# A decoder trunk on one core: x is loaded first, the warming products are laid out anew, tile 0's shift is summed on the tensor engine, and small modulation operations move to ACT

## The chip, the core and the metric

The kernel runs on one core of one Trainium2 chip. A core has a tensor engine (PE, with its weight loads shown as PEld), a vector engine (DVE), a scalar engine (ACT), a general engine (POOL) and a queue engine (SP) that here only issues transfers. Each engine runs its own instructions in order and waits on semaphores of the others. Sixteen DMA engines move data between HBM and the on-chip memory (SBUF); products land in eight banks of PSUM, which PE alone fills and DVE and ACT read. The metric is the device time of one execution in microseconds, as the median of several runs.

## The reference, cut to what matters

One layer of a conditioned decoder: 512 positions, width 1024. The first stage, the only one that the change touches, is the first normalisation with its modulation and the first 768 columns of the input projection:

```python
cs = jax.nn.silu(c)                                  # c: (1, 1024)
mod = cs @ w_ada[l] + b_ada[l]                       # w_ada: 1024 x 6144
shift1, scale1, gate1, shift2, scale2, gate2 = [m[:, None, :] for m in jnp.split(mod, 6, axis=-1)]
h = _rmsnorm(x, norm1_g[l]) * (1.0 + scale1) + shift1
proj = h @ w_in[l]                                   # w_in: 1024 x 4352
qa, ka, va, qd, kd, vd, ga, gd = jnp.split(proj, points, axis=-1)
```

After it come a sliding-window attention, a differential attention, a gated merge with an output projection, and a gated MLP with a short convolution. All is float32.

## The kernel before, in words

A float32 product is made of three products in a reduced format: each operand is split into a high part (a cast, on ACT) and a low part (the difference, on DVE), and high x high, low x high and high x low are summed in PSUM. The first stage walks over the 1024 inputs of the projection in eight tiles of 128 (k = 0 to 7). For each tile it needs three things:

- the normalised and modulated x, transposed: `hTh[k]` (high) and `hTl[k]` (low), each 128 x 512. x lies as four row tiles `xn[:, t]` of 128 positions; PE transposes the four 128 x 128 pieces into the bank `xt` (`h_turn`, line 312), and ACT applies scale and shift while it reads that bank (`h_tile`, line 317), once into `hTh` and once into the float32 copy `hf`; DVE subtracts (`h_low`, line 321);
- the modulation of these 128 inputs: scale and shift, which are columns of `cs @ w_ada`. DVE multiplies the eight 128-row blocks of `adaw` (scale and shift side by side, 256 wide) with the eight columns of `cs` and sums them into `ac` (`ac_ops`, lines 253, 255, 257). PE then sums over partitions by a product with ones into `pa` (line 264), and DVE makes two columns `mod` out of it (lines 273 and 276);
- the 768 columns of the weights, `w0`, split by ACT (lines 296, 297) and DVE (lines 303, 305).

Then PE makes 18 products for the tile, in three parts of six (`mm_k`, line 327): part 0 is high weights x high h, part 1 low weights x high h, part 2 high weights x low h. They go to six banks `acc6` that stay open over all eight tiles. Between part 1 and part 2 of tile k stand the product `pa` and the modulation of tile k+1; the transposes of tile k+1 are issued before part 0 of tile k.

Ahead of the loop, ACT squares the four row tiles with a sum over the row (`stat`, line 345), POOL takes the power -1/2 (line 174), DVE polishes it (lines 180, 184) and scales the first 256 columns of the row tile (line 352); PE transposes tile 0's pieces one by one (`turn`, line 357) with three warming products behind each (`keep_warm`, line 335; 14 more stand before them). The remaining 768 columns are scaled by ACT inside the loop's first turn (line 375).

The order of work of DVE, ACT and PE in this stage is written out by hand (a manual schedule); POOL's and SP's follow from a planner. All large loads are issued by SP in the order of the program: c, tile 0's adaw (two loads of 512 KiB), x (four of 512 KiB), then w0 and adaw alternating, where each adaw waits for one of two buffers. A load also waits until the eighth load before it has landed. POOL makes the constants (identity, ones, the attention masks `dsw` and `ddf`, the scales `qsc`) at the beginning and clears `va` by a memset (line 435); masks, scales and `va` are used only in the attention stage.

Of the kernel before, what the change touches and what calls it, by code (L numbers as in the profile page):

```python
# [14 lines left out]
P = 128  # L15
D = 1024
# [21 lines left out]
WARM = 14  # L38
# [14 lines left out]
def kernel(  # L53
# [85 lines left out]
    qsc = cpool.tile([P, 4], F32, name="qsc")  # L139
    for i in range(4):  # L140
        nc.gpsimd.memset(qsc[0:64, i : i + 1], 2.0 ** (i - 2))
        nc.gpsimd.memset(qsc[64:128, i : i + 1], 2.0 ** (i + 2))

    dsw = cpool.tile([P, 256], F32, name="dsw")
    nc.gpsimd.iota(dsw, [[1, 256]], base=-128, channel_multiplier=-1, allow_small_or_imprecise_dtypes=True)
    nc.gpsimd.affine_select(dsw, dsw, [[-1, 256]], ALU.is_ge, NEG, base=128, channel_multiplier=1)
    nc.gpsimd.affine_select(dsw, dsw, [[1, 256]], ALU.is_gt, NEG, base=0, channel_multiplier=-1)
    ddf = cpool.tile([P, 512], F32, name="ddf")
    nc.gpsimd.iota(ddf, [[1, 512]], base=-384, channel_multiplier=-1, allow_small_or_imprecise_dtypes=True)
    nc.gpsimd.affine_select(ddf, ddf, [[-1, 512]], ALU.is_ge, NEG, base=384, channel_multiplier=1)  # L150
# [3 lines left out]
    nc.sync.dma_start(crow8, c.rearrange("o (a p) -> (o a) p", p=P))  # L154
# [9 lines left out]
    pc8 = tbank("pc8", (P, 8))  # L164
    nc.tensor.transpose(pc8, crow8, ident[:8, :8])
# [36 lines left out]
    def load_ada(g):  # L202
        k, m = g[0], len(g)
        aw = pp.tile([P, 2, KT, m * P], F32, tag="adaw", bufs=2, name=f"adaw{k}")
        for j, base in ((0, D), (1, 0)):
            nc.sync.dma_start(
                aw[:, j], wada[:, base + k * P : base + (k + m) * P].rearrange("(a p) n -> p a n", p=P)
            )
        adaw[k] = aw

    load_ada(groups[0])
    for t in range(NT):
        nc.sync.dma_start(xn[:, t], xd[t * P : (t + 1) * P, :])
    for g in groups:
        if g[0]:
            load_ada(g)
        for k in g:
            r = raw_tile([P, 768], f"w0_{k}")
            nc.sync.dma_start(r, win[k * P : (k + 1) * P, 0:768])
            w0[k] = r  # L220
# [24 lines left out]
    def ac_ops(gi, lo, hi):  # L245
# [10 lines left out]
        if hi == KT:  # L256
            nc.vector.tensor_add(ac[gi][0], ac[gi][0], ac[gi][1])
# [101 lines left out]
    for t in range(NT):  # L359
# [5 lines left out]
        if t == 1:  # L365
            finish_mod(0, reduce_mod(0))
# [1359 lines left out]
```

## Time and profile before

| | us |
|---|---|
| median of 3 runs | 719.99 (719.83 to 721.53) |
| the profiled execution | 722.67 |
| its span | 720.9 |
| first product of tile 0 (line 327) | 19.63 |
| first product of tile 1 | 25.25 |
| first product of tile 2 | 30.59 |
| first product of tile 7 | 57.08 |

The times in the lower half are positions in the span, from the timeline. In a timeline row the first number is the start, the second the duration of the group, then the engine, the line, the operation, what it writes and reads, and how many; in brackets stands how long the engine was idle before it, and what ended that wait. In a row of windows the engines' busy times of a stretch are followed by the granted PE clock (1.00 is full), the share of the DMA engines' time, and the GB/s that they moved.

### The profile page before, as it was taken

Reading aid. Unit: us, or ns where it says so; the run is one execution under the profiler, and the core shown is the slowest. Engines: PE = TensorE matmul, PEld = TensorE weight load, DVE = VectorE, ACT = ScalarE, POOL = GpSimd, SP = SyncE. Lnnn points to the kernel's source line nnn. Section 1 sums busy time; section 2 is a strip of 40 time slices with the busy share of each in tenths; the row PEclk is TensorE's granted clock in tenths of the full one; section 3 lists DMA queues with packets and bytes.
Section 4 is the critical chain, followed back from the end, with each engine's and each line's share of the span. In section 5 each row is a group of like instructions: output and inputs, shape, how many; then the busy total and the mean of one; then the engine's idle time right before and its main releaser. Section 6 shows DMA issues by size and latency. Waiting matters only on the chain. (4 is left out here: it accounts for less than half of the span.)

```text
span 720.9 us, 11252 instructions
## 1 busy us (share of the span) xinstructions
PE 693.5 (96%) x4172; PEld 604.8 (84%) x4172; DVE 589.0 (82%) x1121; ACT 381.5 (53%) x673; POOL 84.7 (12%) x101
## 2 busy tenths in 40 slices
PE   5998899999999999999999999999999999999994
PEld 5776788877887888888889999999999999778883
DVE  5998777887986674875379899888888999889996
ACT  3644656454554233432358666555656666555662
POOL 4000000000100110000012021111111212640000
PEclk8999999999999999999999999999999999999998
DMA  9886222534634565726827698877879769998502
GB/s 303 287 265 195 71 59 61 175 101 133 176 109 155 181 196 179 234 88 210 248 68 147 152 198 206 200 175 212 198 202 217 162 174 253 206 206 220 181 0 118
DMA packets 117367, 124.70 MB, mean 173 GB/s; under 512 B 4511, under 2 KB 93376, under 8 KB 117312
## 3 DMA queue, kind: packets, MB, share of 16 engines
q1 hardware_dynamic: 98254, 97.71, 42.8%
q0 software_dynamic: 18720, 25.73, 20.9%
q8 instruction: 33, 0.54, 0.3%
q10 hardware_dynamic: 338, 0.54, 0.2%
q14 instruction: 22, 0.18, 0.1%
HBM read 121.85 MB, written 2.11 MB: 172 GB/s over the span
## 5 line engine op out<-in xcount | busy, mean ns | idle before, releaser
L1112 PE MATMUL up<-t,m_whi 128*128 128x256 f32 x528 | 96.1, 283 | 0.0
L1112 PEld LDWEIGHTS up<-t,m_whi 128*128 128x128 f32 x528 | 82.4, 192 | 0.0
L1112 PE MATMUL up<-t,m_wlo 128*128 128x256 f32 x264 | 74.7, 283 | 0.1
L1112 PE MATMUL up<-bh,p_wlo 128*128 128x256 f32 x232 | 65.7, 284 | 0.6 <-DVE p_wlo L1055 0.6
L1112 PE MATMUL up<-bh,p_whi 128*128 128x256 f32 x232 | 65.6, 283 | 0.0
L1112 PE MATMUL up<-bl,p_whi 128*128 128x256 f32 x232 | 65.6, 283 | 0.0
L1112 PEld LDWEIGHTS up<-t,m_wlo 128*128 128x128 f32 x264 | 50.6, 192 | 0.3 <-DVE m_wlo L1055 0.3
L1112 PEld LDWEIGHTS up<-bh,p_wlo 128*128 128x128 f32 x232 | 44.4, 192 | 1.1 <-DVE p_wlo L1055 1.1
L748 DVE SCALAR_TENSOR_TENSOR arow<-ra,cs,arow 128x512 f32<-128x512 f32 x56 | 41.9, 748 | 3.9 <-DMA ra<-in_w_ada_dram 3.3
L1112 PEld LDWEIGHTS up<-bh,p_whi 128*128 128x128 f32 x232 | 44.5, 192 | 0.0
L1112 PEld LDWEIGHTS up<-bl,p_whi 128*128 128x128 f32 x232 | 44.5, 192 | 0.0
L1023 POOL DMA_DIRECT2D s<-in_w_up_dram x21 | 27.2, 1385 | 143.2 <-DMA s<-in_w_up_dram 60.1
L1055 DVE TENSOR_TENSOR m_wlo<-s,m_whi 128x1024 fp32r<-128x1024 f32 x31 | 37.8, 1219 | 2.0 <-ACT m_whi L1051 2.0
L1051 ACT CAST m_whi<-s 128x1024 fp32r<-128x1024 f32 x31 | 32.4, 1047 | 9.4 <-DVE s L1045 6.0
L174 POOL TENSOR_TENSOR r<-ms,mhalf 128x1 f32<-128x1 f32 (+1 forms) x16 | 13.5, 844 | 172.9 <-DVE ms L172 106.0
L1112 PE MATMUL up<-t,p_whi 128*128 128x256 f32 x176 | 32.2, 283 | 0.0
L678 ACT ACTIVATE sd<-sd,dmx 128x128 f32<-128x128 f32 (+3 forms) x32 | 17.8, 556 | 22.1 <-DVE dmx L676 15.6
L761 POOL DMA_DIRECT2D mod_rows<-arow x8 | 4.3, 540 | 205.4 <-ACT arow L760 205.2
L1112 PEld LDWEIGHTS up<-t,p_whi 128*128 128x128 f32 x176 | 27.4, 192 | 0.2 <-issue 0.2
L1119 ACT ACTIVATE gT<-a,cv 128x512 f32<-128x512 f32 x22 | 17.7, 814 | 17.7 <-DVE a L1154 17.3
L1051 ACT CAST p_whi<-wa 128x1024 fp32r<-128x1024 f32 x18 | 18.7, 1041 | 12.1 <-PE up L1112 9.0
L1112 PE MATMUL up<-t,p_wlo 128*128 128x256 f32 x88 | 24.9, 283 | 0.0
(476 smaller groups left out, 2125.3 us busy)
## 6 DMA issues: line engine op xcount, KB each, us to landing
ra<-in_w_ada_dram SPq DMA_DIRECT2D x32, 512.0 KB, 4.2
wa<-in_w_up_dram SPq DMA_DIRECT2D x22, 512.0 KB, 4.3
s<-in_w_up_dram SPq DMA_DIRECT2D x21, 512.0 KB, 4.8
s<-in_w_up_dram POOLq DMA_DIRECT2D x21, 512.0 KB, 6.5
adaw<-in_w_ada_dram SPq DMA_DIRECT2D x16, 512.0 KB, 5.1
w<-in_w_in_dram SPq DMA_DIRECT2D x12, 512.0 KB, 4.6
a<-in_w_up_dram SPq DMA_DIRECT2D x11, 512.0 KB, 4.7
b<-in_w_down_dram SPq DMA_DIRECT2D x10, 512.0 KB, 4.3
```

The costliest lines, as they stand in the source:

```text
L174: nc.gpsimd.tensor_tensor(r0, ms, mhalf[:, :n], ALU.pow)
L678: nc.scalar.activation(pm[m], pm[m], AF.Exp, bias=mx[:, m : m + 1], scale=slope, accum_out=lsum[:, m : m + 1])
L748: nc.vector.scalar_tensor_tensor(ac, r[:, a], cc, ac, ALU.mult, ALU.add)
L761: nc.gpsimd.dma_start(mod_rows[idx : idx + 1, hf * S : (hf + 1) * S], row)
L1023: nc.gpsimd.dma_start(dst, upblock(*blk), accum_op=ALU.add)
L1051: nc.scalar.copy(W[J, name][0], R[J, SRC[name]])
L1055: nc.vector.tensor_sub(lo, R[J, SRC[name]], hi.bitcast(F32))
L1112: nc.tensor.matmul(o[u], w[:, k, cu], b[:, k], start=name in ("p1", "m5", "p2") and k == 0 and x == 0, stop=k == 3 and x == 2, skip_group_ ...
L1119: nc.scalar.activation(grow(j), av[J][:, u], AF.Identity, bias=cv[:, 66 + j : 67 + j], scale=cv[:, 44 + j : 45 + j])
```

## The change

Nothing of the result is computed differently in sense. What moves:

1. SP's order of loads: three row tiles of x, tile 0's scale columns in two halves, the last row tile of x in two halves, tile 0's shift columns in three pieces, w0 of tile 0 in two pieces, tile 1's adaw in four pieces, then as before, but with w0 of tile 2 now standing ahead of tile 2's adaw in the queue. c is loaded over ACT's queue, ahead of the bias rows.
2. The constants for the attention (`qsc`, `dsw`, `ddf`) and the memset of `va` are made after the stage's statistics, as POOL's order is now also written by hand.
3. The warming products use ones for both operands and no longer wait for the identity: 4 before c's transpose, 8 behind it, 4 behind each of the first two x tiles, 2 before the first product, in place of 14 and three times 3.
4. For tile 0, DVE sums only the scale half (128 wide); the shift half is eight products on PE straight from `adaw` with a column of `cs`. For tile 1, the last two of eight blocks of both halves go the same way. `pa` is 48 columns wide instead of 1.
5. The two columns of `mod` are made by ACT, with a new column `cb` = (1 + bias) x gain made once on DVE; the bias and gain columns are prepared later, after the second row tile.
6. The statistics of the last row tile come in two halves; the scaling of the other 768 columns (`scale_x`) is spread over ACT's time ahead of the loop.
7. Tile 0's weights: the high part of the 512 query columns is made by DVE, that of the other 256 by ACT; the products of tile 0 begin with the latter (banks 4 and 5).

```diff
-WARM = 14
...
-    nc.sync.dma_start(crow8, c.rearrange("o (a p) -> (o a) p", p=P))
+    nc.scalar.dma_start(crow8, c.rearrange("o (a p) -> (o a) p", p=P))
...
-    load_ada(groups[0])
-    for t in range(NT):
-        nc.sync.dma_start(xn[:, t], xd[t * P : (t + 1) * P, :])
...
+    adaw[0] = pp.tile([P, 2, KT, P], F32, tag="adaw", bufs=2, name="adaw0")
+    for t in range(NT - 1):
+        load_x(t)
+    for lo in (0, 4):
+        load_ada_part(adaw[0], 0, 0, 1, lo, lo + 4)
+    load_x(NT - 1, (0, S, D))
+    for lo, hi in ((0, 4), (4, 6), (6, 8)):
+        load_ada_part(adaw[0], 1, 0, 1, lo, hi)
+    load_w0(0, (512, 768))
+    load_w0(0, (0, 512))
+    for g in groups[1:]:
+        load_ada(g, (0, 4, 8) if g[0] == 1 else (0, 8))
+        load_w0(g[0])
...
+    def keep_warm(n):
+        for i in range(n):
+            nc.tensor.matmul(acc6[5][:, :P], ones, ones, start=True, stop=True)
+
+    keep_warm(4)
+    pc8 = tbank("pc8", (P, 8))
+    nc.tensor.transpose(pc8, crow8, ident[:8, :8])
...
+        js = slice(0, 1 if gi == 0 else 2)
+        for kk in range(lo, min(hi, KT - direct(gi))):
+            a = ac[gi][kk % 2][:, js]
...
+    def direct(gi):
+        return 2 if gi == 1 else 0
+
+    NB = 48
...
+    def mod_mm(pa, aw, j, lo, hi, start):
         for kk in range(lo, hi):
...
+            nc.tensor.matmul(
+                pa[:, j], aw[:, j, kk], cs[:, kk : kk + 1].to_broadcast([P, NB]),
+                start=start and kk == lo, stop=kk == KT - 1,
             )
...
+    def reduce_one(pa, gi, j):
+        more = direct(gi)
+        nc.tensor.matmul(pa[:, j], ac[gi][0][:, j], ones[:, 0:NB], start=True, stop=not more)
+        mod_mm(pa, adaw[gi], j, KT - more, KT, False)
+
+    def finish_one(k, pa, j):
...
+        if j == 0:
+            nc.scalar.activation(m[:, 0:1], pa[:, 0, 0:1], AF.Identity, bias=cb[:, k : k + 1], scale=n1g[:, k : k + 1])
+        else:
+            nc.scalar.activation(m[:, 1:2], pa[:, 1, 0:1], AF.Identity, bias=bsh[:, k : k + 1])
...
-        for i in range(6):
+        for i in (4, 5, 0, 1, 2, 3) if k == 0 else range(6):
...
+    keep_warm(4)
+    stat(2)
+    scale_x(0)
+    ac_ops(0, 0, 4)
+    normalise(2)
+    turn(2)
+    pa0 = pa_bank(0)
+    ac_ops(0, 4, 6)
+    stat(3)
+    ac_ops(0, 6, KT)
+    scale_x(1)
+    mod_mm(pa0, adaw[0], 1, 0, 4, True)
+    mod_mm(pa0, adaw[0], 1, 4, 6, False)
+    ps0 = acc6[3].rearrange("p (j n) -> p j n", j=2)[:, :, 0:NB]
+    reduce_one(ps0, 0, 0)
+    normalise(3)
+    mod_mm(pa0, adaw[0], 1, 6, 8, False)
+    turn(3)
+    wts[0] = tuple(wp.tile([P, 768], F32R, tag=f"w{b}", bufs=WB, name=f"w0{b}0") for b in ("hi", "lo"))
+    nc.scalar.copy(wts[0][0][:, 512:768], w0[0][:, 512:768])
+    finish_one(0, ps0, 0)
+    finish_one(0, pa0, 1)
+    rq, wq, lq = w0_views(0)
+    nc.vector.tensor_copy(wq, rq)
+    split_lo(0, 1)
     h_tile(0)
+    scale_x(2)
+    scale_x(3)
     split_lo(0, 0)
...
                 h_turn(nxt[0])
+                if gi == 0:
+                    keep_warm(2)
             for part in range(3):
                 if part == MOD_AT and k == g[-1] and nxt:
-                    pas = reduce_mod(gi + 1)
+                    pa = pa_bank(nxt[0])
+                    for j in range(2):
+                        reduce_one(pa, gi + 1, j)
+                    for j in range(2):
+                        finish_one(nxt[0], pa, j)
                     split_lo(nxt[0], 0)
-                    finish_mod(gi + 1, pas)
                     split_lo(nxt[0], 1)
...
+    va = big.tile([P, 2, 4, 2 * P], F32R, tag="kvB", name="va")
+    nc.gpsimd.memset(va.bitcast(F32), 0.0)
     man.close()
```

165 lines of the change are left out of this document (70 added, 95 removed).

## The prediction

> **What bounds the kernel now.** The page comes first. TensorE (PE) is busy nearly all the time, and less so in the first fortieth, 18 us.
>
> ```profile
> span 720.9 us, 11252 instructions
> PE 693.5 (96%) x4172; PEld 604.8 (84%) x4172; DVE 589.0 (82%) x1121; ACT 381.5 (53%) x673; POOL 84.7 (12%) x101
> PE   5998899999999999999999999999999999999994
> ```
>
> The change lies wholly in the first 62 us, so I read that stretch by windows, then by the timeline. In the windows' rows the columns are PE, PEld, DVE, ACT, POOL, then granted clock, DMA share, GB/s.
>
> ```profile
> 0.00:5.00 5.00, 0.42 (x2) 0.35 (x2) 0.83 (x5) 1.60 (x3) 4.02 (x22) 1.00 0.55 158
> 5.00:10.00 5.00, 5.00 (x24) 4.98 (x24) 4.43 (x13) 0.58 (x1) 1.50 (x1) 1.00 1.04 347
> 10.00:15.00 5.00, 2.44 (x18) 2.16 (x17) 2.04 (x12) 4.65 (x10) 1.61 (x3) 0.91 1.08 378
> 15.00:19.60 4.60, 4.30 (x19) 3.92 (x19) 4.38 (x16) 0.99 (x3) 0.98 (x2) 0.50 1.10 339
> 30.20:35.60 5.40, 5.35 (x28) 4.17 (x27) 5.21 (x15) 2.32 (x5) 0.00 (x0) 1.00 0.88 278
> ```
>
> Until 19.6 us the DMA engines are full (share 1.04 to 1.10): loads set the pace. In the loop (last row) DVE works 5.21 of 5.40 us and DMA has room again. The timeline of the start:
>
> ```profile
> 1.18 1.03 SPq L206 DMA_DIRECT2D adaw<-in_w_ada_dram  x2
> ...
> 1.48 0.09 POOL L141 MEMSET qsc<- 64x1 f32 x1
> ...
> 4.70 1.80 POOL L435 MEMSET va<- 128x2048 f32 x1
> ...
> 5.35 1.18 DVE L240 TENSOR_SCALAR cols<-cols 128x8 f32<-128x8 f32 x1
> ...
> 6.91 0.62 DVE L253 TENSOR_SCALAR ac<-adaw,cs 128x256 f32<-128x256 f32 x2 [0.36 <-DMA adaw<-in_w_ada_dram]
> ...
> 9.42 1.06 ACT L345 ACTIVATE sq<-xn 128x1024 f32<-128x1024 f32 x1 [6.65 <-DMA xn<-in_x_dram]
> ...
> 12.81 0.33 PE L357 MATMUL xt<-ident,xn 128*128 128x128 f32 x1 [1.71 <-DVE xn L352]
> ...
> 14.19 0.19 ACT L345 ACTIVATION_READ_ACCUMULATOR sq<-xn 128x1 f32 x1
> ...
> 14.29 0.60 ACT L296 CAST w0h<-w 128x512 fp32r<-128x512 f32 x1
> ...
> 15.16 0.15 DVE L170 TENSOR_SCALAR ms<-ss 128x1 f32<-128x1 f32 x1
> ...
> 16.63 0.35 DVE L352 TENSOR_SCALAR xn<-xn,rst 128x256 f32<-128x256 f32 x1
> ...
> 17.06 1.49 PE L335 MATMUL a<-ones,ident 128*128 128x128 f32 x6
> ...
> 18.55 1.06 PE L312 MATMUL xt<-ident,xn 128*128 128x128 f32 x4
> 18.80 0.78 ACT L317 ACTIVATE hThA<-xt,mod 128x512 fp32r<-128x512 f32 x1 [3.61 <-PE xt L357]
> ...
> 19.63 2.23 PE L327 MATMUL a<-hThA,w0h 128*128 128x512 f32 x6
> ```
>
> ACT sits idle 6.65 us until the first x tile lands, because 1 MiB of adaw stands ahead of it. Then come four squares, the statistics, transposes, hThA, and only at 19.63 the first product. Next, one turn of the loop, and its last two starts:
>
> ```profile
> 24.12 0.61 DVE L253 TENSOR_SCALAR ac<-adaw,cs 128x256 f32<-128x256 f32 x2
> ...
> 28.32 0.58 PE L264 MATMUL pa<-ones,ac 128*128 128x1 f32 x4
> ...
> 30.59 1.64 PE L327 MATMUL a<-hThA,w0h 128*128 128x512 f32 x6
> ...
> 32.06 1.54 PE L327 MATMUL a<-hThA,w0l 128*128 128x512 f32 x6
> ...
> 33.43 0.68 DVE L303 TENSOR_TENSOR w0l<-w,w0h 128x512 fp32r<-128x512 f32 x1
> ...
> 33.66 0.58 PE L264 MATMUL pa<-ones,ac 128*128 128x1 f32 x4
> 34.10 1.63 PE L327 MATMUL a<-hTlA,w0h 128*128 128x512 f32 x6
> 34.27 0.22 DVE L273 SCALAR_TENSOR_TENSOR mod<-pa,cols 128x1 f32<-128x1 f32 x1 [0.16 <-PE pa L264]
> 34.41 0.15 DVE L276 TENSOR_TENSOR mod<-pa,cols 128x1 f32<-128x1 f32 x1
> 34.47 0.42 DVE L305 TENSOR_TENSOR w0l<-w,w0h 128x256 fp32r<-128x256 f32 x1
> 34.65 0.78 ACT L317 ACTIVATE hThA<-xt,mod 128x512 fp32r<-128x512 f32 x1 [3.08 <-DVE mod L276]
> 34.81 0.61 DVE L253 TENSOR_SCALAR ac<-adaw,cs 128x256 f32<-128x256 f32 x2
> ...
> 35.56 0.60 PE L312 MATMUL xt<-ident,xn 128*128 128x128 f32 x4
> 35.92 1.64 PE L327 MATMUL a<-hThA,w0h 128*128 128x512 f32 x6
> ...
> 52.02 1.64 PE L327 MATMUL a<-hThB,w0h 128*128 128x512 f32 x6
> ...
> 57.08 1.56 PE L327 MATMUL a<-hThB,w0h 128*128 128x512 f32 x6
> 58.48 1.56 PE L327 MATMUL a<-hThB,w0l 128*128 128x512 f32 x6
> ```
>
> A turn lasts 5.33 us (30.59 to 35.92). DVE waits only 0.16 us in it (for pa) and is the bound; PE is close behind.
>
> **The change, part by part: loads.** I turn the GB/s rows into bytes moved: 0.79 MB at 5.0, 2.53 at 10, 4.42 at 15, 5.98 at 19.6. One MiB is 1.05 MB. Adaw's first MiB was moved at 5.75 and landed at 6.9, 1.2 us later; the cast of w0 (3.54 MB, moved at 12.7) started at 14.29 without a wait, so its lag was at most 1.6. The changed order starts its large loads at the head of SP's queue, where c stood (c goes to ACT's queue), some 0.4 us earlier. With a lag of 1.2 to 1.6: the last half of x (2.62 MB, moved at 10.2) lands at 11.0 to 11.4; tile 0's shift weights (3.15 MB) at 12.4 to 12.8; w0 (3.54) at 13.5 to 13.9; tile 1's adaw (4.59) at 16.2 to 16.6. Tile 2's adaw comes at 6.42 MB, since w0 of tiles 1 and 2 now go ahead of it: at the 339 GB/s of the row before, moved at 20.9, landed at 21.7 to 22.1; I take 21.9. The pieces are smaller (15 issues in place of 10), but about 1.4 MB is always queued, so I cost the extra issues at nothing.
>
> **Statistics and first product.** x3's two half squares are an estimate of 0.55 us each (half of 1.06). From the last half: square and accumulator read 0.75, to 11.95; ms to the end of the scaled head took 15.16 to 16.98, 1.82, giving 13.8; transposes about 0.6; hThA 0.8 and a handover: 15.2. PE's queue has tile 1's four transposes (1.06) and two warming products ahead of the first product. Three of these took 1.49 at half clock, so two take 0.5 to 1.0, and the first product starts at about 16.1, against 19.63. The squares of x0 to x2 and scale_x(0) and (1) fill ACT's waits for later x tiles. The mod columns are needed on ACT by 14.4; the shift's eight products follow their weights (12.8) by two or three of pa's 0.44 us, so they fit. Making w0's high part on DVE (a 512-wide copy, 0.4 to 0.7 by the 512-wide CAST and TENSOR_TENSOR rows) takes 1.0 us of casts off ACT, less the 256-wide one that stays.
>
> **Tile 1.** DVE after 13.8: copy 0.6, two low parts 1.0, six ac operations 2.2, the low part of h and the sum 1.1: 18.7. PE: 16.1 plus two parts (30.59 to the earliest end of the second, 1.47 + 1.40 = 2.87) is 19.0. pa has six products in place of two, three times 0.44 = 1.3; then 1.46 and 0.36. Tile 1's first product: 22.1, against 25.25.
>
> **Tile 2, where gain is given back.** DVE would be free for ac(2) at 19.7, but adaw lands at 21.9: that is the new wait, behind which h_low and the low parts of w0 queue. From ac(2) to pa took 24.12 to 28.32, 4.2, and from pa to the next tile's start 28.32 to 30.59, 2.27. So tile 2 starts at 28.4, against 30.59: 2.2 us earlier.
>
> **The loop.** Two DVE operations per tile go to ACT. From L303 to L305 it was 1.04 us; without them about the 0.6 that L303's issue needs: DVE's turn falls to 4.9. PE's turn is then the bound: 1.47 + 1.40 (57.08 to 58.48, undisturbed) + 0.44 + 1.46 + 0.36 = 5.13 to 5.15. ACT's two small operations are not in the trace in this form. Nearest below is DVE's 0.15 to 0.22, nearest above the 1.18 that L240 shows; I take 0.2, as both normal neighbours are there. hThA then starts where it did, about 1.0 after pa, and ends 0.4 before PE needs it, so they cost nothing; at over 0.4 each they would show. Each of the four turns from tile 2 to tile 6 gains about 0.2, and the last (52.02 to 57.08 before, 5.06; no transposes in it, 5.15 - 0.36 = 4.79 after) 0.27: 1.0 in all. Wider pa (48 columns) hides in its weight loads.
>
> **Constants.** qsc, dsw, ddf and va's memset, 5.0 us of POOL (1.48 to 6.50 before), now run after x3's power, from about 13.1 to 18.1; nobody needs them before 60 us. The row at 5.35 shows the danger: DVE's 128x8 operation took 1.18 beside va's memset, ending at 6.53, just behind it. At 13.8 to 18.1 DVE's only plain copy falls beside the short qsc memsets, so zero by the near rows, up to 4.3 if everything waits for POOL.
> By the Trainium skill ("SBUF — State Buffer", section "Who interferes with whom"), an operation of DVE that uses both port pairs waits out a GpSimd operation completely, and one with two SBUF inputs waits only for one that reads SBUF. The trace agrees (1.18 beside va). This speaks against moving the constants here, and is a rival below.
>
> **Sum.** 2.2 at tile 2 plus 1.0 in the loop = 3.2 us. What follows (evacuation at 60 us, products that PE bounds) has the same instruction order and moves as a block. The profiled execution took 722.67 us (span 720.9 plus 1.8 around it), 2.7 above the median of 719.99; I carry the difference alone: 719.99 - 3.2 = 716.8.
>
> **Rivals.**
> *The clock stays at half.* The row from 15 to 19.6 shows 0.50, after no wait of PE longer than 1.71 us. The changed PE has waits of that size between transposes. If it is at half clock from 16.1 to 20.6, tile 0's first two parts take 5.1 in place of 2.87: pa(1) at 21.2, tile 1 at 24.4, tile 2 at 29.5 (24.4 + 2.87 + 2.27), and with the loop's 1.0 the gain is 2.1: 717.9. For: the same pattern before. Against: warming products now stand between all transposes.
> By the Trainium skill ("TensorE: Matmul & The Clock Gate", section "Part 1: The HAM clock gate (the "warmup" mystery)") the clock falls only after an idle window of about 3.4 us. By that no gap here would lower it, and the sum stays 716.8. The trace differs: it fell behind gaps of 1.7 us.
>
> *No wait for tile 2's adaw.* If it lands by 19.7, PE bounds tile 1 too (22.1 + 2.87 + 2.27 = 27.2): 1.2 more, 715.6. For: rates of 378 at 10 to 15 us. Against: 339 as soon as adaw is in the stream.
>
> *The constants block DVE.* All of DVE's work after 13.8 waits for 18.1: the sum of tile 1 at 23.0, ac(2) at 23.9, tile 2 at 30.4; gain 0.2 + 1.0: 718.8.
>
> *Slower: the stream of small pieces runs slower.* Place: SP's first 17 loads, each waiting for the eighth before it. The forecast turns into a loss over 0.3% when ac(2) starts after 27.3 (21.9 + 3.2 + 2.2), that is 6.42 MB at under about 270 GB/s from 2.5 us on. At 250 it starts at 29.4 and the time is 724.3. For: 158 in the first five us, and 278 in the loop. Against: in the loop DVE paces the loads; wherever loads were queued, the rows show 339 to 378.
>
> **How the numbers follow.** A measurement of this kernel tells about 0.3%, 2.2 us, from no change. The forecast (716.8, own range 715.9 to 717.8) 0.53; no wait 0.15; half clock 0.15; constants 0.08; slower stream 0.09. Faster: 0.53 + 0.15 = 0.68. Same: 0.23. Slower: 0.09. The range takes in no wait below with 0.4 for the loads' lag, and half clock and constants above: 715.2 to 718.9; left out are the slower stream and some edges.
>
> **What would show it.** x0's square starts at about 5 us, not 9.4; first product at 16, tile 1 at 22, tile 2 at 28.4, tile 7 at 53.8; a DVE wait for adaw of some 2 us before ac(2); turns of 5.15 with PE free of waits; ACT's mod operations 0.2 each. The forecast is wrong if the clock row at 16 to 21 us stays at 0.5, if pieces land at under 300 GB/s, or if the stages after 62 us do not move with the first one.

## The result: slower by 0.44%, and the profile after

The changed kernel takes 724.11 us (721.97 to 726.09) where the kernel before, measured beside it, takes 720.39 (718.76 to 722.46): a ratio of 1.0044 with an interval of 1.0029 to 1.0059. The forecast was 716.8, with a range up to 718.9: the sign is wrong.

The page of the changed kernel (span, engines, and PE's busy tenths in 40 slices):

```profile
span 719.9 us, 11298 instructions
...
PE 694.2 (96%) x4192; PEld 605.4 (84%) x4192; DVE 585.7 (81%) x1106; ACT 386.0 (54%) x690; POOL 84.6 (12%) x101
...
PE   8899899999998999999999999999999999999994
```

The first slice of PE went from 5 to 8 tenths, and the span from 720.9 to 719.9. By these lines the change looks like a small gain. It is not, since the profile of before that I had read was a long execution of that kernel: 722.67 us, where its median is about 720.4. A second profile of it (720.08 us, span 718.3, called "before, again" below) is the fairer partner, with one reserve: at 370 us PE waits 1.68 us for DVE in it, where no other profile loses more than 0.4. Distances to it that are given below for places before 370 us therefore don't add up to the difference of the spans. The start in rows of the timeline, first of the changed kernel:

```profile
4.31 1.06 ACT L354 ACTIVATE sq<-xn 128x1024 f32<-128x1024 f32 x1 [0.69 <-DMA xn<-in_x_dram]
...
13.89 0.35 ACT L289 ACTIVATE mod<-a,cb,cols 128x1 f32<-128x1 f32 x1 [0.91 <-PE a L281]
...
16.28 2.47 PE L341 MATMUL a<-hThA,w0hi 128*128 128x512 f32 x6
...
17.45 1.81 POOL L466 MEMSET va<- 128x2048 f32 x1
...
22.58 0.62 DVE L257 TENSOR_SCALAR ac<-adaw,cs 128x256 f32<-128x256 f32 x2 [2.53 <-DMA adaw<-in_w_ada_dram]
...
23.04 1.66 PE L341 MATMUL a<-hThA,w0h 128*128 128x512 f32 x6
...
27.43 0.35 ACT L289 ACTIVATE mod<-pa,cb,cols 128x1 f32<-128x1 f32 x1 [3.21 <-PE pa L281]
27.68 0.25 ACT L291 ACTIVATE mod<-pa,cols 128x1 f32<-128x1 f32 x1
...
29.03 0.62 DVE L257 TENSOR_SCALAR ac<-adaw,cs 128x256 f32<-128x256 f32 x2 [1.46 <-DMA adaw<-in_w_ada_dram]
...
29.06 1.64 PE L341 MATMUL a<-hThA,w0h 128*128 128x512 f32 x6
...
35.49 1.64 PE L341 MATMUL a<-hThA,w0h 128*128 128x512 f32 x6
...
55.72 1.67 PE L341 MATMUL a<-hThB,w0h 128*128 128x512 f32 x6 [0.21 <-ACT hThB L331]
...
60.65 0.50 PE L117 MATMUL pq<-hThA,w_h 128*128 128x512 f32 x1 [0.46 <-DVE qa L483]
```

and of before, again:

```profile
18.57 1.66 PE L327 MATMUL a<-hThA,w0h 128*128 128x512 f32 x6 [0.43 <-ACT hThA L317]
...
24.04 1.66 PE L327 MATMUL a<-hThA,w0h 128*128 128x512 f32 x6 [0.16 <-ACT hThA L317]
...
29.12 1.64 PE L327 MATMUL a<-hThA,w0h 128*128 128x512 f32 x6
...
34.47 1.64 PE L327 MATMUL a<-hThA,w0h 128*128 128x512 f32 x6
...
55.61 1.58 PE L327 MATMUL a<-hThB,w0h 128*128 128x512 f32 x6
...
60.44 0.50 PE L118 MATMUL pq<-hThA,w_h 128*128 128x512 f32 x1 [0.47 <-DVE qa L428]
```

Tile 0 starts 2.3 us earlier (16.28 against 18.57) and tile 1 1.0; tile 2 starts level (29.06, 29.12) and tile 3 1.0 later. The loop wins most of that back; the first product after the stage stands 0.2 later. The brackets of two rows show why: DVE waits twice for tile weights of the modulation, 2.53 us ahead of tile 2's sums and 1.46 ahead of tile 3's. The windows of the changed kernel (columns as in the prediction):

```profile
10.00:15.00 5.00, 3.36 (x26) 2.85 (x25) 4.71 (x21) 3.44 (x9) 2.47 (x11) 0.97 1.15 308
15.00:20.00 5.00, 5.00 (x22) 4.29 (x20) 5.00 (x11) 3.66 (x6) 4.04 (x6) 0.69 1.11 334
```

and of before, again:

```profile
10.00:15.00 5.00, 2.88 (x21) 2.61 (x20) 2.50 (x16) 4.12 (x8) 2.28 (x4) 0.89 1.09 371
15.00:20.00 5.00, 4.57 (x24) 4.11 (x24) 4.86 (x14) 2.26 (x5) 0.30 (x1) 0.76 1.10 368
```

The DMA engines are as busy as before (1.15 and 1.11 of their time) but move 308 and 334 GB/s instead of 371 and 368. So the stage brings nothing. That explains a missing gain, not a loss of 2 to 3.7 us; the rest had to be found later in the program, where the change edits nothing.

### The profile page after: what moved, and what is told of

The parts are those of the page before. It is cut to its first block, busy times and chain, and to the rows that moved or that the text cites. A ratio compares the mean times of both kernels' runs of the same rounds, so it can differ in the third digit from the quotient of the medians.

```text
span 719.9 us, 11298 instructions
## 1 busy us (share of the span) xinstructions
PE 694.2 (96%) x4192; PEld 605.4 (84%) x4192; DVE 585.7 (81%) x1106; ACT 386.0 (54%) x690; POOL 84.6 (12%) x101
## 5 line engine op out<-in xcount | busy, mean ns | idle before, releaser
L159 POOL TENSOR_TENSOR r<-ms,mhalf 128x1 f32<-128x1 f32 (+1 forms) x16 | 12.7, 795 | 177.3 <-DVE ms L157 107.1
```

Source lines behind the costliest of these rows:

```text
L159: nc.gpsimd.tensor_tensor(r0, ms, mhalf[:, :n], ALU.pow)
```

## The experiments

Two theories stood at first. By the one, the loss arises in the first stage (the order or the pieces of the loads, the constants on POOL, the granted clock). By the other, it arises later, from something that the first stage shifts. The second took shape when I set the same PE instructions of two traces beside each other: in the changed kernel's first profile their distance to before, again hardly moves from 62 to 170 us (0.2 at both ends) and then grows in steps, most of it between 185 and 232 us.

### The same kernels again

before_same is the kernel before, after_same and after_same2 are the changed one, all with no edit.

> The kernel before, unchanged, once more, for the spans and clocks of its executions. Its earlier profile had a span of 720.9 us, 2.3 above what its usual time leaves (720.4 less 1.8). Theory A (what is lost lies behind the first stage, in stretches at half clock): most executions here show a span near 718.6 and a mean clock above the 0.988 of the earlier profile, about 0.992. Theory B (what is lost lies in stages whose pace the loads set): spans near 718.6 with the same clock as the changed kernel's executions, about 0.989.

> The changed kernel, unchanged, once more. 0.3 to 0.6% above the kernel before. Theory A: a second stretch at half clock stands in the clock row of this profile whenever its mean clock is below 0.992, and the instructions behind it come 1.7 to 2.6 us later than in the earlier profile of this kernel. Theory B: the clock row is as in the earlier profile, and the loss lies at 180 to 270 us, in a wait for a load.

> The changed kernel once more, beside the three that differ from it in one part. 722.8 to 724.1 us, mean clock about 0.990; if its profile shows a mean clock of 0.990 or less, then by theory A two or three stretches at half clock stand at 12 to 22 us, and tile 1 starts at 24 to 26 us in place of 23.

Measured: 720.44 us (ratio to the runs beside it 0.9995, 0.9978 to 1.0012); 722.82 (1.0040, 1.0022 to 1.0058); 722.24 (1.0031, 1.0015 to 1.0046). The loss is real and lies between 2.0 and 3.7 us. after_same starts its tiles 0, 1 and 2 at 16.30, 23.06 and 29.67. after_same2 shows, for tile 1, the rival of the half clock as it was drawn up:

```profile
16.99 2.91 PE L341 MATMUL a<-hThA,w0hi 128*128 128x512 f32 x6
...
24.38 1.65 PE L341 MATMUL a<-hThA,w0h 128*128 128x512 f32 x6
...
29.65 1.64 PE L341 MATMUL a<-hThA,w0h 128*128 128x512 f32 x6
```

```profile
13.40:20.00 6.60, 6.49 (x24) 5.62 (x24) 6.12 (x16) 4.86 (x9) 5.23 (x13) 0.50 1.12 324
68.00:71.30 3.30, 3.30 (x17) 2.25 (x16) 2.15 (x13) 0.00 (x0) 0.00 (x0) 0.50 0.54 161
```

The rival had tile 1 at 24.4 and tile 2 at 29.5. That tile 2 agrees too is luck: after_same has a single half-clock window and starts it at 29.67. In both, DVE gets tile 2's adaw only at 23.2 us, and tile 2 starts 6.5 us later. So theory A's marks are there in after_same2 (two windows at 13 to 20 us, tile 1 above 24), and a loss at the place that theory B names is there in after_same (0.9 us between 185 and 232). The half clock itself occurs in some executions and not in others: the mean granted clock is 0.990 and 0.991 over the runs of after_same and after_same2, and 0.993 over those of before_same. A half-clock window of 3.4 us takes 0.0024 off a run's mean, so the changed kernel has on average about one more of them. What that costs stands in the sum at the end of the section on why the prediction was wrong.

### Parts of the change undone or exaggerated

const_early makes POOL's constants and the memset at the beginning, as before:

```diff
+    qsc = cpool.tile([P, 4], F32, name="qsc")
...
+    va = big.tile([P, 2, 4, 2 * P], F32R, tag="kvB", name="va")
...
-    man.enter_context(tc.manual_schedule(engines={nc.vector.engine, nc.scalar.engine, nc.tensor.engine, nc.gpsimd.engine}))
+    man.enter_context(tc.manual_schedule(engines={nc.vector.engine, nc.scalar.engine, nc.tensor.engine}))
...
+    nc.gpsimd.memset(va.bitcast(F32), 0.0)
```

> The changed kernel with the attention's constants and the clearing of va made by POOL where the kernel before made them. By my prediction's step (constants behind the statistics cost nothing) the same as the changed kernel within 0.1%, the ten products before 20 us unmoved. Rival (POOL beside DVE slows the operations of DVE there): ac(1) takes 0.61 per pair in place of 0.96, tile 1 starts 0.5 to 1.0 us earlier, tile 2 not at all, since it waits for its load.

Measured: 722.85 us, 1.0038 (1.0023 to 1.0054), as after_same in the same comparison (722.82). Where the constants stand is worth nothing that can be told from these runs, though the slowdown that the rival fears is there. The first two operations of tile 1's sums on DVE, in the changed kernel beside POOL's work on the constants, and in const_early without it:

```profile
15.28 0.96 DVE L257 TENSOR_SCALAR ac<-adaw,cs 128x256 f32<-128x256 f32 x2
```

```profile
15.95 0.61 DVE L269 TENSOR_SCALAR ac<-adaw,cs 128x256 f32<-128x256 f32 x2
```

From tile 0's start to tile 1's it is 6.76 us in the one and 6.75 in the other.

big_pieces keeps the new order of loads and loads each in one piece:

```diff
-    for lo in (0, 4):
-        load_ada_part(adaw[0], 0, 0, 1, lo, lo + 4)
-    load_x(NT - 1, (0, S, D))
...
+    load_ada_part(adaw[0], 0, 0, 1, 0, 8)
+    load_x(NT - 1)
...
-        load_ada(g, (0, 4, 8) if g[0] == 1 else (0, 8))
+        load_ada(g)
```

> The changed kernel's order of loads, but each in one piece as before (the scale and the shift columns of tile 0, the last row tile, w0 of tile 0, and tile 1's adaw): six loads fewer. My rival of the prediction (small pieces run slower): ac(2) starts before 21.5 us in place of 22.6, and the time falls by 1 us or more. If only the bytes ahead of tile 2's adaw count: ac(2) starts at 22.2 to 22.9 again; tile 0 starts some 0.5 to 1 us later, as its last pieces land later; the time stays within 0.15%.

Measured: 725.74 us, 1.0070 (1.0044 to 1.0096), 2.9 above after_same, though the two intervals just overlap. Tile 2's sums start at 24.08 us, not before 21.5. The small pieces help rather than harm; the rival that the prediction set on the slower side has its sign reversed.

w_behind makes SP issue the loads from tile 1 on in the program's order, so that tile 2's weights no longer stand ahead of its adaw:

```diff
+    inorder = ExitStack()
+    inorder.enter_context(tc.manual_schedule(engines={nc.sync.engine}))
     for g in groups[1:]:
         load_ada(g, (0, 4, 8) if g[0] == 1 else (0, 8))
         load_w0(g[0])
...
+    inorder.close()
```

> The changed kernel with SP's loads from tile 1 on in the order of the program: tile 2's adaw ahead of tile 2's w0, tile 3's ahead of tile 3's and 4's. If the bytes ahead of adaw set the pace of the first tiles: tile 2's adaw lands some 1 us earlier (0.39 MB at 330 GB/s is 1.2), ac(2) starts at 21.4 to 22.2 in place of 22.6 to 23.2, tile 3 at about 34.4 in place of 35.4, and the time falls by 0.5 to 1 us. If not (the loads are slow for another reason, or w0 becomes the late one): tile 3 at 35.4 again and the time within 0.1%.

Measured: 723.36 us, 1.0048 (1.0034 to 1.0062). Tile 2's sums start at 21.81, as the first branch has it, but PE had two half-clock windows (13.5 to 20.3 us) and tile 2 starts at 29.64 all the same. Tile 3 starts at 35.34, as in the changed kernel, and no gain shows. In this profile the clock stands in the way, so the order of these two loads is not tested by itself.

after_warm adds four warming products at three places (behind the third tile's transposes, ahead of the scale sum, behind the last transposes):

```diff
     turn(2)
+    keep_warm(4)
...
     turn(3)
+    keep_warm(4)
```

> The changed kernel with 12 warming products more, four each in TensorE's waits at 11.5 to 14.5 us. Theory A (stretches at half clock cost the changed kernel more than the kernel before; its mean clock was 0.990 against 0.993): no half clock at 14 to 18 us, mean clock up to 0.993 to 0.997, the time 1 us lower. If the clock at the start doesn't matter, since loads set the pace there: the same time within 0.1%, whatever the clock.

Measured: 724.93 us, 1.0065 (1.0042 to 1.0088). The profile shows half clock from 12.2 to 22.5 us. More warming at these places does not hold the clock: the mean over the runs is 0.990, as in after_same.

x_second loads tile 0's adaw ahead of x, with all the rest of the change in place:

```diff
+    for lo in (0, 4):
+        load_ada_part(adaw[0], 0, 0, 1, lo, lo + 4)
+    for lo, hi in ((0, 4), (4, 6), (6, 8)):
+        load_ada_part(adaw[0], 1, 0, 1, lo, hi)
     for t in range(NT - 1):
         load_x(t)
-    for lo in (0, 4):
-        load_ada_part(adaw[0], 0, 0, 1, lo, lo + 4)
     load_x(NT - 1, (0, S, D))
-    for lo, hi in ((0, 4), (4, 6), (6, 8)):
-        load_ada_part(adaw[0], 1, 0, 1, lo, hi)
```

> The changed kernel with tile 0's adaw loaded ahead of x again; all else as changed. By my prediction's step (x first brings the first product 3.5 us forward, and tile 2 2.2 us): tile 0 at 18.5 to 20 us, tile 2 at 30 to 31, time 1.5 to 2.2 us above the changed kernel. By theory E (tile 2's and later starts are set by the bytes ahead of their adaw, which are the same): tile 0 later by 2 to 3 us, tile 1 by 1 to 2, but tiles 3 to 7 within 0.5 us of the changed kernel, time within 0.15% of it.

Measured: 727.29 us, 1.0093 (1.0073 to 1.0113), 5.0 above after_same2 beside it. Its tiles 0 and 1:

```profile
22.81 2.46 PE L341 MATMUL a<-hThA,w0hi 128*128 128x512 f32 x6
...
29.58 1.65 PE L341 MATMUL a<-hThA,w0h 128*128 128x512 f32 x6
```

The start does reach the end: a stage that begins 6 us later costs 5 us. Part of that is clock, since PE does nothing from 7.5 to 10.9 us in this profile, has half clock from 10.9 to 24.6, and the runs' mean clock is 0.987 against 0.991. Both expectations missed, the one of 1.5 to 2.2 us by its size, and the one that nothing would change altogether; with it fell the theory that the first stage is hidden. "x first" is worth having within this change.

### The length of TensorE's program

The change also makes PE's program longer: 45 instructions more in the first stage, 24 of them ahead of the loop. The trace of before shows 33 packets of 16 KB on the queue named q8 instruction, over the whole span. I take them for PE's program, fetched piece by piece: the page counts 8344 products and weight loads on PE, and 33 packets of 256 instructions are 8448. Three kernels test whether the place of these fetches matters. They put products of 8 x 8 numbers, which nobody reads, in front of the warming; as compiled, each is four instructions.

before_pad adds 11 of them to the kernel before (44 instructions, about what the change adds), before_pad32 adds 32 and before_pad64 adds 64 in the same place:

```diff
+    for i in range(11):
+        nc.tensor.matmul(acc6[5][:8, :8], ones[:, :8], ones[:, :8], start=True, stop=True)
```

> The kernel before with 11 tiny products more (8 x 8) ahead of the first warming products, where TensorE waits for the identity: 44 TensorE instructions more, so that the fetches of its program, one of 16 KB for every 256 instructions, fall where they fall in the changed kernel (which has 45 more). Theory C (the stages behind the first lose 2 us because each fetch occupies one DMA engine for about 1 us, and now hits loads on which the end waits): the first stage as before, then TensorE falls behind by 0.4 to 0.6 us at 173, 0.5 at 198, 0.5 to 1.0 at 221 us, and the time rises by 1 to 2 us, to about 721.5 to 722.5. Theory D (those steps come from something else in the changed start): no steps, 720.4 within 0.15%.

> The kernel before with 64 tiny products more at its start, where there were 11: 256 TensorE instructions, one whole block, so that the fetches behind the first stage fall where they fall in the kernel before. Theory C (the place of the fetches costs the time): DVE's waits for the row write of the modulation are three of together 4.4 to 4.6 us again, not four of 6.9 as with 11 products; no steps at 189, 198 and 221 us; 720.4 us, or up to 0.7 less if the clock stays full at the start. Theory D (the added products themselves bring the loss, through the clock or the start): about 722.0 as with 11 of them.

> The kernel before with 32 tiny products at its start: 128 TensorE instructions, half a block. Fetches then fall some 11 us earlier in the work than in the kernel before, about 173 and 195 us in place of 184 and 206, and none stands beside the row write at 180 us. Theory C: DVE's wait behind that row write is 0.3 us as in the kernel before, not 1.9 as with 11 products, no step at 189 us, and the time is 719.5 to 721, unless the fetch hits another transfer that the end waits for. Theory D (any added products that leave the old place cost): 721.5 to 722.5, as with 11.

Measured: before_pad 722.02 us, 1.0019 (1.0009 to 1.0029); before_pad64 720.55, 1.0006 (0.9992 to 1.0020); before_pad32 721.83, 1.0010 (0.9993 to 1.0028). Eleven products of next to no work make the kernel before slower by 1.6 us, and 64 of them by less than can be told; 32 lie between and can't be told from either. With 64 the program is one packet longer, and every later fetch is back in its old place; before_pad, then before_pad64:

```profile
q8 instruction: 33, 0.54, 0.3%
```

```profile
q8 instruction: 34, 0.56, 0.3%
```

What a fetch meets in its new place is a write of 2 KB to HBM (`mod_rows`, a row of the later modulation), for which DVE waits before it overwrites `arow`. The write's issue and DVE's next operation in before_pad:

```profile
180.83 0.55 POOL L763 DMA_DIRECT2D mod_rows<-arow  x1 [11.79 <-ACT arow L762]
...
184.18 0.49 DVE L748 TENSOR_SCALAR arow<-ra,cs 128x512 f32<-128x512 f32 x1 [1.95 <-DMA mod_rows<-arow]
```

in before_pad64:

```profile
181.52 0.55 POOL L763 DMA_DIRECT2D mod_rows<-arow  x1 [11.79 <-ACT arow L762]
...
183.16 0.48 DVE L748 TENSOR_SCALAR arow<-ra,cs 128x512 f32<-128x512 f32 x1 [0.28 <-DMA mod_rows<-arow]
```

and in after_same2:

```profile
180.57 0.55 POOL L815 DMA_DIRECT2D mod_rows<-arow  x1 [11.79 <-ACT arow L814]
...
183.69 0.49 DVE L800 TENSOR_SCALAR arow<-ra,cs 128x512 f32<-128x512 f32 x1 [1.74 <-DMA mod_rows<-arow]
```

That the fetch is what delays the write shows in its parts: in before_pad a fetch starts 1.31 us after the write's issue, 15 of the write's 16 parts land 1.45 to 1.61 us after that issue, and the last at 3.33; in before_pad64 all 16 land by 1.62. DVE waits 1.95 and 1.74 us in place of 0.28, and everything behind that on its queue comes later, up to the operands of four transposes on PE at 222 us. Two groups of products, ahead of the place and behind it, measure what this costs PE; in before, again (170.73 to 222.54, 51.81 us):

```profile
170.73 0.95 PE L125 MATMUL sd<-qkv 64*128 64x128 f32 x12
...
222.54 0.63 PE L693 MATMUL td<-ident,sd 128*128 128x128 f32 x4 [0.33 <-DVE sd L684]
```

in before_pad (53.49 us):

```profile
172.91 0.95 PE L125 MATMUL sd<-qkv 64*128 64x128 f32 x12
...
226.40 0.63 PE L695 MATMUL td<-ident,sd 128*128 128x128 f32 x4 [1.03 <-DVE sd L686]
```

in after_same2 (53.78 us):

```profile
172.62 0.96 PE L124 MATMUL sd<-qkv 64*128 64x128 f32 x12
...
226.40 0.63 PE L747 MATMUL td<-ident,sd 128*128 128x128 f32 x4 [1.52 <-DVE sd L738]
```

The kernel whose only edit is 44 idle instructions loses 1.7 us in this stretch, the changed one 2.0, and both end it on a wait for DVE. before_pad64 loses nothing here (the table below). Its time is a weaker witness than its trace: its runs had a mean clock of 0.9957, against 0.9929 for those beside it, and its profile lies 2.8 us behind before, again already at 100 us. The 64 products may thus cost something at the start and gain something by the clock; no run here tells the two apart. Now the changed kernel with its fetches moved back. after_pad adds 23 and 30 tiny products at two places (212 instructions, 257 with the change's 45; `pad(n)` is n of the products above); tiny, the second diff, puts 65 of them in place of 12 warming products (257 again):

```diff
+    pad(23)
     keep_warm(4)
...
+    pad(30)
     keep_warm(8)
```

```diff
-    keep_warm(4)
     nc.tensor.transpose(pc8, crow8, ident[:8, :8])
+    for i in range(65):
+        nc.tensor.matmul(acc6[5][:8, :8], ones[:, :8], ones[:, :8], start=True, stop=True)
...
-    keep_warm(8)
```

> The changed kernel with 53 tiny products more (8 x 8) among the first warming products: 212 TensorE instructions, which with the 45 of the change make one whole block of 256, so that all later fetches fall where they fall in the kernel before. Theory C: the steps at 173, 198, 221 and 252 us are gone, and the time falls by 1 to 2 us, less what the products cost at the start (0 to 1 us). Theory D: the steps stay; the time stays or rises by up to 1 us.

> The changed kernel with 65 tiny products behind c's transpose in place of the first twelve warming products: the TensorE program is then longer than that of the kernel before by a whole block (257 instructions against 256), and c's columns are not delayed. Theory C: waits for the row write 4.4 to 4.7 us in three, time 1.3 to 1.7 us below the changed kernel of this call, about 721.5. Theory A on top (tiny products at the start went with a clock of 0.993 and more): another 0.5 to 1 us. Neither: as the changed kernel.

Measured: after_pad 722.78 us, 1.0043 (1.0027 to 1.0058): no gain, a miss for the theory. tiny 721.49, 1.0011 (0.9997 to 1.0024), 0.75 below after_same2 beside it, with intervals that overlap, and at a higher mean clock (0.9945 against 0.9907), so that its time alone does not speak for the theory. DVE's wait is back at 0.25 and 0.26, and in tiny the stretch takes 51.85 us again:

```profile
172.45 0.96 PE L124 MATMUL sd<-qkv 64*128 64x128 f32 x12
...
224.30 0.63 PE L747 MATMUL td<-ident,sd 128*128 128x128 f32 x4 [0.32 <-DVE sd L738]
```

In after_pad PE still loses 1.2 us between 185 and 232, at another point (195 to 202); its cause I did not find.

### A third buffer for adaw

Do the two waits for adaw in the first stage come with its two buffers? adaw3 gives the changed kernel three, before_adaw3 the kernel before; adaw3_pad and adaw3_tiny are after_pad and tiny with three, and adaw3_tiny33 has 33 tiny products in place of 65:

```diff
-        aw = adaw[k] = pp.tile([P, 2, KT, m * P], F32, tag="adaw", bufs=2, name=f"adaw{k}")
+        aw = adaw[k] = pp.tile([P, 2, KT, m * P], F32, tag="adaw", bufs=3, name=f"adaw{k}")
```

> The changed kernel with three buffers for adaw in place of two, so that no load of adaw waits for DVE to have read the one before the last, and tile 2's adaw stands ahead of tile 2's w0 in the queue. Theory E (the first stage is bound by the loads of adaw, and that is where the 3.2 us of my sum went): no DVE wait for adaw over 0.5 us from tile 3 on; tile 2's adaw lands at 21.0 to 22.0; turns of 5.05 us; tile 7 at 52.5 to 54 us in place of 55.7 to 58, and the time 1.5 to 3 us less than the changed kernel's 723. Against it (the loads' rate is the bound, not the buffers): tile 2 at 28.5 to 29.5 again, tile 7 at 55 or later, the time within 0.1% of 723.

> The kernel before with three buffers for adaw in place of two. Its loop is paced by DVE (turns of 5.33 us, no wait for adaw): by theory E the third buffer brings it nothing, 720.4 within 0.15%, tiles 2 to 7 at turns of 5.33. If the loads set its pace too: turns of 5.1 and 1 us less.

> The changed kernel with three buffers for adaw and the 53 tiny products that make up a whole block of TensorE instructions: both causes taken away at once. Theories C and E together: DVE's waits for the row write 4.4 to 4.6 us in three, tile 7 at 53 to 55 us (the products cost up to 1 us at the start), 719 to 720.5 us, which would be no slower than the kernel before. If one of them is wrong: 721 to 723.

> The same with three buffers for adaw. All causes found so far are taken away: tile 2 at 27.5 to 28.5 us, tile 7 at 53 to 54.5 us, no waits for adaw beyond tile 2's. If the sum of my prediction was right apart from these causes: 717.5 to 719.5 us, below the kernel before. If the first tiles stay bound by the loads or the clock: 720 to 721, as with the first trial.

> The changed kernel with three buffers for adaw and 33 tiny products behind c's transpose in place of the first twelve warming products: half a block fewer than with 65, which gave 719.5. Theory C: no fetch beside the row write at 180 us (wait behind it 0.3 us) and the first columns of c not delayed: 718.5 to 720, below the kernel before. If the shorter row of products lets the clock fall for longer (mean under 0.990) or other transfers are hit: 720 to 722.

Measured: adaw3 722.28 us, 1.0034 (1.0019 to 1.0048); before_adaw3 721.19, 1.0015 (1.0003 to 1.0027); adaw3_pad 720.90, 1.0011 (0.9997 to 1.0025); adaw3_tiny 719.54, 0.9988 (0.9976 to 1.0000); adaw3_tiny33 720.72, 1.0012 (0.9996 to 1.0028). Starts of tiles 0 to 3 in adaw3_tiny:

```profile
16.77 2.43 PE L342 MATMUL a<-hThA,w0hi 128*128 128x512 f32 x6
...
23.59 1.65 PE L342 MATMUL a<-hThA,w0h 128*128 128x512 f32 x6
...
29.18 1.64 PE L342 MATMUL a<-hThA,w0h 128*128 128x512 f32 x6
...
34.22 1.66 PE L342 MATMUL a<-hThA,w0h 128*128 128x512 f32 x6
```

Tile 3 starts 1.3 us earlier than in the changed kernel: the second wait is gone, the first (1.48 us) is not. The kernel before gains nothing from the buffer. adaw3 alone missed what was expected of it: tile 7 starts at 55.86 us, not at 52.5 to 54, and no gain of 1.5 us shows; its profile has half clock from 11.5 to 21.7 us. adaw3_tiny misses its starts too (tile 2 at 29.18, tile 7 at 55.15), and adaw3_pad and adaw3_tiny33 lie 0.4 and 0.7 us above their hoped-for ranges. With the fetches out of the way the times differ by 1.95 us for the third buffer (tiny to adaw3_tiny, of which 0.4 is time outside the span), and by 1.4 for the place of the fetches in its presence (adaw3 to adaw3_pad, with a mean clock of 0.990 and 0.992). adaw3_tiny is the fastest, 2.7 us below the changed kernel beside it, and 0.7 below the kernel before, which its interval just fails to tell from nothing.

### All kernels in one table

Column 2 is the number of PE instructions in the first stage beyond those of before; column 3 the time from the issue of the row write to the start of the nearest fetch; column 4 DVE's wait behind that write; column 5 how much the distance of the same PE instructions to before, again grew from 185 to 232 us; all in us, from one profile each.

| kernel | added | fetch | DVE wait | growth | ratio of times |
|---|---|---|---|---|---|
| before, first profile | 0 | +4.54 | 0.42 | -0.02 | 1 |
| before, again | 0 | +4.61 | 0.27 | 0 | 0.9995 |
| before_adaw3 | 0 | +4.62 | 0.23 | 0.00 | 1.0015 |
| before_pad64 | 256 | +4.69 | 0.28 | -0.01 | 1.0006 |
| tiny | 257 | +4.48 | 0.26 | -0.01 | 1.0011 |
| adaw3_pad | 257 | +4.42 | 0.27 | -0.07 | 1.0011 |
| adaw3_tiny | 257 | +4.45 | 0.28 | 0.66 | 0.9988 |
| after_pad | 257 | +4.48 | 0.25 | 1.19 | 1.0043 |
| adaw3_tiny33 | 129 | -3.86 | 0.25 | 0.22 | 1.0012 |
| before_pad | 44 | +1.31 | 1.95 | 1.58 | 1.0019 |
| before_pad32 | 128 | +1.01 | 1.92 | 0.91 | 1.0010 |
| after | 45 | +0.89 | 1.65 | 1.67 | 1.0044 |
| after_same | 45 | +0.81 | 1.52 | 0.92 | 1.0040 |
| after_same2 | 45 | +0.90 | 1.74 | 1.88 | 1.0031 |
| const_early | 45 | +1.31 | 1.93 | 2.00 | 1.0038 |
| big_pieces | 45 | +1.11 | 1.75 | 1.31 | 1.0070 |
| w_behind | 45 | +1.37 | 2.04 | 2.35 | 1.0048 |
| after_warm | 93 | +0.98 | 1.91 | 1.12 | 1.0065 |
| adaw3 | 45 | +0.88 | 1.80 | 2.01 | 1.0034 |
| x_second | 45 | +1.03 | 1.70 | 1.62 | 1.0093 |

Wherever a fetch starts 0.8 to 1.4 us after the row write, DVE waits 1.5 to 2.0 us; elsewhere 0.2 to 0.4, without an exception. The next row write, 25 to 26 us later, meets a fetch in nine of the kernels (0.7 to 1.4 us after its issue): it lands after 2.8 to 3.5 us instead of 1.6, and DVE waits for it another 0.5 to 1.2 us. The growth is 0.9 to 2.35 us in the first case and, after_pad apart, -0.1 to 0.7 in the second. The expectation for before_pad32, that no fetch would meet the write, was wrong: where a fetch falls I could not work out from the count alone. The wait that then followed fits, but its time (1.0010) shows no loss that can be told.

## Why the prediction was wrong, point by point

**x first, tile 0: right.** x0's square at 4.31 us ("about 5"), the first product at 16.28 (16.1). Against the fair partner that is 2.3 us earlier, not 3.5, and x_second shows that the start counts.

**Tile 1: mis-sized.** 23.04 against 22.1. Half clock ran in part of 15 to 20 us (0.69 in the window), where part 0 alone took 2.47 us in place of the 1.47 that the sum used.

**Tile 2 and the loads: half right.** I had one wait, of about 2 us, with adaw at 21.9. It was 2.53, to 22.58, and from there tile 2 took 6.48 us to start, as worked out (4.2 and 2.27). The failed term is the one behind it: I let the loop run on without waits, but tile 3's adaw is late too (1.46 us, to 29.03), and tile 3 starts at 35.49, where 28.4 and a turn of 5.15 make 33.55. The rate that I carried over from before (339 GB/s) was 308 and 334 here.

**The loop: right in its turns, little use.** From tile 3 to tile 7 it is 20.23 us; three turns of 5.15 and a last one of 4.79 are 20.24. ACT's two small operations took 0.35 and 0.25 us, not 0.2 each, and cost nothing, as forecast.

**Tile 7 and the gain of 3.2: wrong on both sides.** Tile 7 starts at 55.72 instead of 53.8, 1.9 late, and before, again starts it at 55.61, not 57.08: 1.5 of the gain was never there. 3.2 - 1.9 - 1.5 is -0.2, about what the rows show at 60 us (60.65 against 60.44). The step "I carry the difference alone" took a long execution's start for the median's. Its 0.50 row at 15 to 19.6 us and its 2.7 us above the median had both been quoted; once PE has reached full clock, before, again loses it in this stage only from 13.9 to 17.4 us. A second half-clock window of that long execution, at 68.7 us, cost it another 1.4 us and lay outside the stage.

**Constants: right in the time, not in the reason.** No loss or gain can be told (const_early). But it was not only the plain copy that stood at risk: two operations of tile 1's sums took 0.96 us beside POOL in place of 0.61.

**"What follows ... has the same instruction order and moves as a block": the step that turned the sign.** The order is the same, but the program's place in its 16 KB packets is not. before_pad, in which nothing but that place and 44 idle instructions is changed, loses 1.6 us (0.09% to 0.29% of the time), and its profile loses 1.58 from 185 to 232 us; in the changed kernel's three profiles the same stretch loses 0.9 to 1.9 us. So the term for what follows, which the sum put at nothing, was about 1 to 2 us.

**The rivals.** Half clock came true in some executions, with tile 1 at the start worked out for it; tile 2 agreed by luck. What the prediction set against it was not so: no warming product stands between the transposes of the third and the fourth row tile. "No wait" fell. The constants slow DVE a little, without effect on the time. The slower stream of small pieces fell: whole pieces are slower by 2.9 us. No rival looked beyond 62 us, and so none had the right sign for the right reason.

**The sum, as far as it goes.** Of the loss of 2.0 to 3.7 us: the first stage 0.2 to 0.6 (the distance at 62 us in the three profiles); the stretch of the row writes 0.9 to 1.9; outside the span 0.35 (below). Half clock comes on top. after_same2 has two windows more than after_same and lies 1.57 us further behind at 100 us, but only 0.1 at 62 us: the window in the first stage costs next to nothing, the one at 68 us most of the rest. The executions on record tell how much is left at the same clock. Where the mean clock is 0.993 or 0.994, 75 executions of the kernel before average 720.2 us and nine of the changed one 722.2; at 0.989 to 0.991 they average 721.3 (24 executions) and 723.3 (19). About 2.0 us of the loss thus remain at equal clock, and some 0.9 of the 2.9 by which all these executions differ go with the lower clock. This compares executions and is no experiment on the clock. How the 2.0 us divide is not closed: a further 0.4 to 0.7 us is lost shortly before 180 us in four of the variants (after and after_same among them), and 0.1 to 0.9 between 240 and 260 us in all variants of the changed kernel, with 0 to 0.3 in those of before; the causes are open.

## What to carry to other kernels

Before a gain is carried from one profile to a median, the profile's own distance from the median has to be explained; here more than half of it sat in the very stage that the change rebuilds. In a kernel of 10,000 instructions an edit at the start also moves every later program fetch, so an effect of 0.2 to 0.4% should be tried against the same kernel with a few idle instructions added. And a load that is pulled forward pushes others back: ask of each later tile, not only of the next, when its data lands.

## What the runs showed of the hardware

**Program fetches share the DMA engines with the data.** PE's program comes in packets of 16 KB (33 packets, 0.54 MB; 256 more instructions make 34). A packet takes 0.9 to 2 us. Where one starts 0.7 to 1.4 us after the issue of one of the two row writes, the write lands 1.2 to 1.9 us late; in before_pad it is one of its 16 parts that is late, which fits a fetch that holds one of the sixteen DMA engines. By the Trainium skill ("Runtime: NRT & Kernel Launch", section "Instruction fetch mechanics") the program is streamed in blocks of 16 KiB, 256 instructions, and the cost of crossing from one to the next is mostly hidden. The trace agrees on the size; on the cost it differs where a short transfer that somebody waits for is met: DVE's wait for 2 KB goes from 0.2 to 0.4 us up to 1.5 to 2.0.

**The clock.** The clock rows show 1.00 from the start of the span, but PE starts at half clock: in before, again the passes of the warming products (two each) follow one another by 213 ns up to 10.5 us, by 111 from then to 12.7, and by 213 again in the half-clock window behind; in after_same the first change comes at 7.2 us. Until the first recorded change the row says nothing. After that, half clock comes in windows of 3.4 us whose places differ between executions of the same kernel. By the Trainium skill ("TensorE: Matmul & The Clock Gate", section "Part 1: The HAM clock gate (the "warmup" mystery)") the window is free-running and what a kernel gets of it varies from run to run; the trace agrees with that, with 13.3 to 20.1 us in after_same2 beside a single window in this stage in after_same (14.0 to 17.4). The same section lets the clock fall after an idle window. x_second agrees: its clock falls behind 3.4 us in which PE did nothing. In the other profiles it fell behind windows in which PE was busy for 0.45 to 0.83 of the time, and others with the same share did not lower it. after_warm shows three windows in a row with twelve more warming products, but big_pieces and adaw3 do so without them. Of the kernels with tiny products at the start, before_pad, before_pad64, after_pad and adaw3_tiny33 show none before 30 us, while before_pad32, tiny, adaw3_pad and adaw3_tiny show one or two. What decides it stays open.

**Outside the span.** The time of a run beyond its span is 2.1 to 2.2 us in after, after_same, after_same2, const_early, big_pieces, tiny and x_second, and about 1.8 in the others. The first are those whose last program packet, on the second instruction queue (q14), starts 1.5 us or more after the span's end. That these go together is all that was seen.
